# Average pooling over runs of four: where a group's rows lie in memory, and which queue stores them

## The chip, the cores and the metric

The kernel runs on one NeuronCore of a Trainium2 chip. The metric is the device time of one execution in microseconds (us); lower is better. A core has several engines with instruction streams of their own: VectorE (DVE in the profile), ScalarE (ACT), GpSimd (POOL), SyncE (SP) and TensorE (PE). Sixteen DMA engines move data between the chip's main memory (HBM) and the on-chip memory (SBUF, 128 partitions). An engine that issues a transfer puts it into its own DMA queue: here SP has one (q1 in the profile) and ScalarE another (q10), and both are served by the same sixteen DMA engines.

## The reference

```python
def setup_inputs():
    return {
        "x": np.random.randn(64, 256, 8192).astype(np.float32),
        "kernel_size": 4,
        "stride": 4,
    }

def reference(x, kernel_size, stride):
    batch, channels, length = x.shape
    out_len = (length - kernel_size) // stride + 1
    output = np.zeros((batch, channels, out_len), dtype=np.float32)
    for i in range(out_len):
        start = i * stride
        output[:, :, i] = np.mean(x[:, :, start : start + kernel_size], axis=2)
    return output
```

Every four neighbouring values of the input become their mean. Windows do not overlap and no window crosses a row, so the whole input may be treated as one long line of numbers: 536.87 MB in, 134.22 MB out.

## The kernel before

The input is cut into 64 blocks of 8.39 MB. A block is 128 partitions of RUN = 16384 numbers, 64 KB each, and one block is one contiguous stretch of HBM: partition p's 64 KB follow those of partition p-1 (`xb`, L35). Its result is 128 partitions of M = 4096 numbers, 16 KB each, again one contiguous stretch (`ob`, L36).

For each block, `load` (L41 to L45) issues one transfer on SP's queue into an input tile `xt`. There are two input tiles (L38), so a load has to wait until VectorE has finished with the block two before. `sums` (L47 to L56) is two additions on VectorE: L50 adds neighbours, 16384 to 8192 numbers, and writes over the first half of `xt`; L54 adds neighbours again, 8192 to 4096, and writes half of a result tile `r`. A result tile holds two blocks, and there are two of them (L39). `scale` (L58, L59) multiplies by 1/4 on ScalarE, in place.

The order around the stores:

- The blocks go in pairs (L68). In the first eight blocks (SINGLES, L11) each block is scaled and stored by itself, with 16 KB per partition, by ScalarE's queue (L73 to L75).
- From the ninth block on, a pair is scaled in one instruction of 128 x 8192 numbers (L77) and stored by one transfer of 4096 KB on ScalarE's queue (L78). The function `both` (L65) gives its place in HBM: two blocks, so two separate runs of 16 KB for each partition.
- The last pair but one is scaled after the last loads have been issued, and stored on SP's queue (L86, L87). The last two blocks are stored singly on SP's queue (L90, L95), the very last in two pieces: its load, sums, scale and store are cut by LAST (L12) into 10240 and 6144 numbers.

Waits between engines are inserted by the framework from the tiles that an instruction reads and writes. Each engine runs its instructions in the order written, so an instruction that waits holds up those behind it on that engine. SP does nothing but issue transfers.

Of the kernel before, what the change touches and what calls it, by code (L numbers as in the profile page):

```python
# [1 line left out]

# [4 lines left out]


RUN = 16384

SINGLES = 8  # L11
LAST = (10240, 6144)  # L12


@with_exitstack
def kernel(
    ctx: ExitStack,
    tc: tile.TileContext,
    x: bass.AP,
    kernel_size: bass.AP,  # L20
    stride: bass.AP,
    out: bass.AP,
):
    nc = tc.nc
    K, S = int(kernel_size), int(stride)
    assert K == S == 4
    B, C, L = x.shape
    P = nc.NUM_PARTITIONS
    dt = x.dtype
    M = RUN // K  # L30
    blocks = B * C * L // (P * RUN)
    assert blocks * P * RUN == B * C * L and L % K == 0 and blocks % 2 == 0
    assert sum(LAST) == RUN

    xb = x.rearrange("b c l -> (b c l)").rearrange("(n p m) -> n p m", p=P, m=RUN)  # L35
    ob = out.rearrange("b c l -> (b c l)").rearrange("(n p m) -> n p m", p=P, m=M)  # L36

    pin = ctx.enter_context(tc.tile_pool(name="xin", bufs=2))  # L38
    pout = ctx.enter_context(tc.tile_pool(name="res", bufs=2))  # L39

    def load(i, a=0, b=RUN, xt=None):  # L41
        if xt is None:
            xt = pin.tile([P, RUN], dt, name="xt")
        nc.sync.dma_start(out=xt[:, a:b], in_=xb[i][:, a:b])
        return xt  # L45

    def sums(o, xt, a=0, b=RUN):  # L47
        v = xt[:, a:b].rearrange("p (m k) -> p m k", k=2)
        h = xt[:, a : (a + b) // 2]
        nc.vector.tensor_tensor(  # L50
            out=h, in0=v[:, :, 0], in1=v[:, :, 1], op=mybir.AluOpType.add
        )
        w = h.rearrange("p (m k) -> p m k", k=2)
        nc.vector.tensor_tensor(  # L54
            out=o, in0=w[:, :, 0], in1=w[:, :, 1], op=mybir.AluOpType.add
        )  # L56

    def scale(o):  # L58
        nc.scalar.mul(o, o, 1.0 / K)  # L59

    def edges(cuts):
        at = [sum(cuts[:j]) for j in range(len(cuts) + 1)]
        return list(zip(at[:-1], at[1:]))

    def both(i):  # L65
        return ob[i : i + 2].rearrange("n p m -> p n m")

    for i in range(0, blocks - 2, 2):  # L68
        r = pout.tile([P, 2, M], dt, name="r")
        for h in range(2):  # L70
            xt = load(i + h)
            sums(r[:, h, :], xt)
            if i < SINGLES:  # L73
                scale(r[:, h, :])
                nc.scalar.dma_start(out=ob[i + h], in_=r[:, h, :])  # L75
        if SINGLES <= i < blocks - 4:
            scale(r[:])  # L77
            nc.scalar.dma_start(out=both(i), in_=r[:])  # L78

    n = blocks - 1  # L80
    t = pout.tile([P, 2, M], dt, name="r")
    xt = load(n - 1)
    xl = None
    for a, b in edges(LAST):
        xl = load(n, a, b, xl)
    scale(r[:])  # L86
    nc.sync.dma_start(out=both(n - 3), in_=r[:])  # L87
    sums(t[:, 0, :], xt)
    scale(t[:, 0, :])
    nc.sync.dma_start(out=ob[n - 1], in_=t[:, 0, :])  # L90
    for a, b in edges(LAST):
        o = t[:, 1, a // K : b // K]
        sums(o, xl, a, b)
        scale(o)
        nc.sync.dma_start(out=ob[n][:, a // K : b // K], in_=o)  # L95


# [1 line left out]
_INS = ['x', 'kernel_size', 'stride']  # L99
_OUTS = [((64, 256, 2048), 'float32')]  # L100

_NUMBERS = {'kernel_size': 4, 'stride': 4}


# [26 lines left out]
```

## Time and profile before

| what | value |
|---|---|
| median of 3 runs | 1554.86 us (1554.7 to 1556.03) |
| the profiled execution | 1554.4 us, of which its span 1552.6 us |
| VectorE busy | 839.7 us (54%) |
| ScalarE busy | 227.4 us (15%) |
| one L50 of 128 x 8192, one L54 of 128 x 4096 | 8692 ns, 4425 ns |
| one L59 of 128 x 4096, of 128 x 8192 | 3616 ns, 7029 ns |
| HBM read and written | 536.87 MB and 134.22 MB, 432 GB/s over the span |
| issue to landing, median: load | 35.1 us |
| issue to landing, median: store of 2048 KB, of 4096 KB on ScalarE's queue | 31.7 us, 52.0 us |
| issue to landing: store of 4096 KB on SP's queue (L87) | 33.0 us |

The span is the time that the trace covers; the execution's own time is 1.8 us longer. "Busy" counts computing instructions only. A DMA engine handles a transfer as a row of packets, and a packet here is one contiguous run in HBM and in one partition: 64 KB for a load's partition, 16 KB for a store's. In lists of instructions in order of time the columns are start, length, engine, line, operation, what it writes and reads, and in brackets the idle time before it with what ended it. In lists of waits they are who waited for whom, the sum in us, how many times, and the longest.

### The profile page before, as it was taken

To read this page: it belongs to the slowest core of one execution; us is meant where nothing else is said; L and a number is where in the kernel's file an instruction comes from. 1 tells how busy PE (TensorE), PEld (TensorE's weight loads), DVE (VectorE), ACT (ScalarE), POOL (GpSimd) and SP (SyncE) were. 2 spreads that over 40 slices of the span, in tenths; PEclk is the share of its full clock that TensorE was granted. 3 is DMA by queue.
4 is the path that set the end of the run, shared out by engine and by line. 5 is a ranking of instruction groups with operands and counts; after the bars stand their busy time and mean duration, and the time that the engine had idled before them with its cause. 6 is when DMAs were issued, how large, how long until landed. Compare 5 with 4: busy or idle time off the path is not lost.

```text
span 1552.6 us, 471 instructions
## 1 busy us (share of the span) xinstructions
DVE 839.7 (54%) x130; ACT 227.4 (15%) x39; POOL 0.2 (0%) x4
## 2 busy tenths in 40 slices
DVE  3646556546465464654646546455464554645646
ACT  1111101110111101111011110111101111011111
POOL 0000000000000000000000000000000000000000
DMA  9999999999999999999999999999999999999999
GB/s 417 420 434 438 439 439 439 412 445 444 413 433 435 443 438 439 432 424 429 439 438 433 437 434 419 439 432 438 439 419 434 434 437 439 441 423 442 422 440 400
DMA packets 18292, 671.12 MB, mean 432 GB/s; under 512 B 1649, under 2 KB 1649, under 8 KB 1777
## 3 DMA queue, kind: packets, MB, share of 16 engines
q1 hardware_dynamic: 10064, 545.26, 81.1%
q10 hardware_dynamic: 8224, 125.83, 18.9%
q14 instruction: 4, 0.02, 0.0%
HBM read 536.87 MB, written 134.22 MB: 432 GB/s over the span
## 4 chain that ended last, share of the span: by engine, by line
DMA 71%; DVE 28%; issue 0%; ACT 0%; DVEq 0%
DMA xt<-in_x_dram 71%; DVE xt L50 18%; DVE r L54 9%; ACT r L59 0%; DVEq L54 0%
## 5 line engine op out<-in xcount | busy, mean ns | idle before, releaser
L50 DVE TENSOR_TENSOR xt<-xt 128x8192 f32<-128x8192 f32 (+1 forms) x65 | 556.5, 8561 | 696.1 <-DMA xt<-in_x_dram 696.1
L59 ACT ACTIVATE r<-r 128x8192 f32<-128x8192 f32 (+3 forms) x38 | 226.2, 5951 | 1313.0 <-DVE r L54 1313.0
L54 DVE TENSOR_TENSOR r<-xt 128x4096 f32<-128x4096 f32 (+1 forms) x65 | 283.4, 4360 | 3.9
L59 ACT ACT_TABLE_LOAD x1 | 1.3, 1283 | 0.7 <-PEq L112 0.7
L112 POOL MEMSET const-bfloat16-1.0<- 128x1 bf16 x1 | 0.1, 101 | 0.0
L112 POOL MEMSET const-uint8-127<- 128x1 uint8 x1 | 0.1, 101 | 0.0
L112 POOL MEMSET const-float32-0.0<- 128x1 f32 x1 | 0.1, 98 | 0.2 <-issue 0.2
L112 POOL MEMSET const-float32-1.0<- 128x1 f32 x1 | 0.1, 98 | 0.0
## 6 DMA issues: line engine op xcount, KB each, us to landing
out_dram<-r ACTq DMA_DIRECT2D x26, 4096.0 KB, 52.0
out_dram<-r ACTq DMA_DIRECT2D x8, 2048.0 KB, 31.7
xt<-in_x_dram SPq DMA_DIRECT2D x1, 5120.0 KB, 23.1
out_dram<-r SPq DMA_DIRECT2D x1, 4096.0 KB, 33.0
xt<-in_x_dram SPq DMA_DIRECT2D x1, 3072.0 KB, 30.0
out_dram<-r SPq DMA_DIRECT2D x1, 2048.0 KB, 16.9
out_dram<-r SPq DMA_DIRECT2D x1, 1280.0 KB, 12.9
xt<-in_x_dram SPq DMA_DIRECT2D x63, 35.1
```

What stands on the lines that cost most here:

```text
L50: nc.vector.tensor_tensor(out=h, in0=v[:, :, 0], in1=v[:, :, 1], op=mybir.AluOpType.add)
L54: nc.vector.tensor_tensor(out=o, in0=w[:, :, 0], in1=w[:, :, 1], op=mybir.AluOpType.add)
L59: nc.scalar.mul(o, o, 1.0 / K)
L112: nc = _bacc.Bacc("TRN2", target_bir_lowering=False, num_devices=1)
```

## The change

Blocks are replaced by groups of two halves. A group is 128 partitions with 128 KB of contiguous input each; half h of a group is the h-th 64 KB of every partition. A load still moves 64 KB for each of 128 partitions, but the rows of one load lie 128 KB apart in HBM rather than 64 KB. The two results of a partition then lie side by side in HBM, 32 KB in one run, so that a whole group is stored with one run per partition.

The first four groups (eight halves) are stored by halves on ScalarE's queue, with 16 KB per partition, 32 KB apart. From the fifth group on, each half is scaled by itself, nothing is stored by ScalarE, and SP issues the group's store (`store`, 4096 KB, 32 KB per partition) in the next group, behind the load of that group's second half. The group and its tile are kept in `held` until then. The end is ordered as before: the last loads, the held group, the last group's first half, and its second half in two pieces, all on SP's queue.

```diff
-SINGLES = 8
+SINGLES = 4
...
-    xb = x.rearrange("b c l -> (b c l)").rearrange("(n p m) -> n p m", p=P, m=RUN)
-    ob = out.rearrange("b c l -> (b c l)").rearrange("(n p m) -> n p m", p=P, m=M)
+    xb = x.rearrange("b c l -> (b c l)").rearrange(
+        "(n p h m) -> n h p m", p=P, h=2, m=RUN
+    )
+    ob = out.rearrange("b c l -> (b c l)").rearrange(
+        "(n p m) -> n p m", p=P, m=2 * M
+    )
...
-        nc.sync.dma_start(out=xt[:, a:b], in_=xb[i][:, a:b])
+        nc.sync.dma_start(out=xt[:, a:b], in_=xb[g, h][:, a:b])
...
-    def both(i):
-        return ob[i : i + 2].rearrange("n p m -> p n m")
+    def store(g, r, a=0, b=2 * M):
+        nc.sync.dma_start(out=ob[g][:, a:b], in_=r[:, a:b])
 
-    for i in range(0, blocks - 2, 2):
-        r = pout.tile([P, 2, M], dt, name="r")
-        for h in range(2):
-            xt = load(i + h)
-            sums(r[:, h, :], xt)
-            if i < SINGLES:
-                scale(r[:, h, :])
-                nc.scalar.dma_start(out=ob[i + h], in_=r[:, h, :])
-        if SINGLES <= i < blocks - 4:
-            scale(r[:])
-            nc.scalar.dma_start(out=both(i), in_=r[:])
+    def half(g, r, h):
+        o = r[:, h * M : (h + 1) * M]
+        nc.scalar.dma_start(out=ob[g][:, h * M : (h + 1) * M], in_=o)
 
-    n = blocks - 1
-    t = pout.tile([P, 2, M], dt, name="r")
-    xt = load(n - 1)
+    held = None
+    for g in range(groups):
+        r = pout.tile([P, 2 * M], dt, name="r")
+        xt = load(g, 0)
+        sums(r[:, :M], xt)
+        scale(r[:, :M])
+        if g == groups - 1:
+            break
+        if g < SINGLES:
+            half(g, r, 0)
+        xt = load(g, 1)
+        if held is not None:
+            store(*held)
+        sums(r[:, M:], xt)
+        scale(r[:, M:])
+        if g < SINGLES:
+            half(g, r, 1)
+        else:
+            held = g, r
+
     xl = None
     for a, b in edges(LAST):
-        xl = load(n, a, b, xl)
-    scale(r[:])
-    nc.sync.dma_start(out=both(n - 3), in_=r[:])
-    sums(t[:, 0, :], xt)
-    scale(t[:, 0, :])
-    nc.sync.dma_start(out=ob[n - 1], in_=t[:, 0, :])
+        xl = load(g, 1, a, b, xl)
+    store(*held)
+    store(g, r, 0, M)
     for a, b in edges(LAST):
-        o = t[:, 1, a // K : b // K]
-        sums(o, xl, a, b)
-        scale(o)
-        nc.sync.dma_start(out=ob[n][:, a // K : b // K], in_=o)
+        a1, b1 = M + a // K, M + b // K
+        sums(r[:, a1:b1], xl, a, b)
+        scale(r[:, a1:b1])
+        store(g, r, a1, b1)
```

In the changed file `load` is at L45 to L49 (the transfer at L48), the two additions at L54 and L58, the scale at L63, and the transfers of `store` and `half` at L70 and L74.

More of the change, by code (lines that the diff above doesn't have):

```diff
@@ L30, with load @@
     M = RUN // K
-    blocks = B * C * L // (P * RUN)
-    assert blocks * P * RUN == B * C * L and L % K == 0 and blocks % 2 == 0
+    groups = B * C * L // (2 * P * RUN)
+    assert groups * 2 * P * RUN == B * C * L and L % K == 0
     assert sum(LAST) == RUN
-    xb = x.rearrange("b c l -> (b c l)").rearrange("(n p m) -> n p m", p=P, m=RUN)
-    ob = out.rearrange("b c l -> (b c l)").rearrange("(n p m) -> n p m", p=P, m=M)
+    xb = x.rearrange("b c l -> (b c l)").rearrange(
[4 more added lines that the diff above has]
+    )
     pin = ctx.enter_context(tc.tile_pool(name="xin", bufs=2))
     pout = ctx.enter_context(tc.tile_pool(name="res", bufs=2))
-    def load(i, a=0, b=RUN, xt=None):
+    def load(g, h, a=0, b=RUN, xt=None):
         if xt is None:
             xt = pin.tile([P, RUN], dt, name="xt")
-        nc.sync.dma_start(out=xt[:, a:b], in_=xb[i][:, a:b])
+        nc.sync.dma_start(out=xt[:, a:b], in_=xb[g, h][:, a:b])
         return xt
```

## The prediction

> **What bounds the kernel now.** I read the page's stripes and queues first, then the chain, then the waits of VectorE and of SP, then the order of time in the middle and at the end. The queues on the page:
>
> ```profile
> DMA  9999999999999999999999999999999999999999
> DMA packets 18292, 671.12 MB, mean 432 GB/s; under 512 B 1649, under 2 KB 1649, under 8 KB 1777
> q1 hardware_dynamic: 10064, 545.26, 81.1%
> q10 hardware_dynamic: 8224, 125.83, 18.9%
> ...
> DMA 71%; DVE 28%; issue 0%; ACT 0%; DVEq 0%
> ```
>
> The 16 DMA engines are full in every slice, and the shares of the two queues (q1 is SP's, q10 ACT's) add up to 100% of the span. The chain's 28% of VectorE is misleading: it follows single waits through two input buffers, and says nothing of whether the DMA engines had other work meanwhile. The waits:
>
> ```profile
> ACT r L59 <- DVE r L54: 1313.0, 38, 44.8
> DVE xt L50 <- DMA xt<-in_x_dram: 696.1, 63, 22.7
> ...
> SPq L44 <- DVE r L54: 817.2, 62, 13.2
> SPq L44 <- DMA xt<-in_x_dram: 660.1, 62, 21.1
> ```
>
> VectorE waits for 63 loads, 11 us each; ScalarE waits for VectorE. SP waits up to 13.2 us for the sums to free a buffer, but it then issues a load behind one still running. The middle, in order of time (start, length):
>
> ```profile
> 400.29 8.69 DVE L50 TENSOR_TENSOR xt<-xt 128x8192 f32<-128x8192 f32 x1 [11.14 <-DMA xt<-in_x_dram]
> 409.07 4.43 DVE L54 TENSOR_TENSOR r<-xt 128x4096 f32<-128x4096 f32 x1
> 424.43 8.69 DVE L50 TENSOR_TENSOR xt<-xt 128x8192 f32<-128x8192 f32 x1 [10.93 <-DMA xt<-in_x_dram]
> 433.15 4.43 DVE L54 TENSOR_TENSOR r<-xt 128x4096 f32<-128x4096 f32 x1
> 437.62 7.03 ACT L59 ACTIVATE r<-r 128x8192 f32<-128x8192 f32 x1 [41.40 <-DVE r L54]
> 444.67 0.38 ACTq L78 DMA_DIRECT2D out_dram<-r  x1
> 448.65 8.69 DVE L50 TENSOR_TENSOR xt<-xt 128x8192 f32<-128x8192 f32 x1 [11.07 <-DMA xt<-in_x_dram]
> ```
>
> A pair takes 48.36 us (400.29 to 448.65) for 16.78 MB in and 4.19 MB out: 434 GB/s. Loads alone run no faster: VectorE's first two starts, 22.73 and 42.06, are 19.33 us apart for 8.39 MB, again 434 GB/s. So reads, writes and mixtures share one rate, and only bytes, packets and gaps count.
>
> No view prints packets singly, so I read the trace's packet records themselves. On one engine the next packet starts 2.414 us after a 64 KB packet, 0.607 after 16 KB, 0.381 after 10 KB, 0.231 after 6 KB, and 0.006 after a semaphore write. Each engine serves 128/16 = 8 partitions, so a load is 8 packets of 64 KB and a pair's store 16 of 16 KB. One engine's sum: 63 whole loads are 504 x 2.414 = 1216.7; the last, of 40 KB and 24 KB pieces at 1.510 and 0.908, 19.3; 16 KB stores, 64 in the singles, 416 in 26 pairs and 24 at the end, 504 x 0.607 = 305.9; the two last pieces 4.9; 103 semaphores 0.6. Together 1547.4 us. The first packets start at 3.0 to 3.8 us and the last ends with the span, 1552.6. Everything slower than these steps sums to 1.3 us per engine, 0.7 of it in the very first packets, 0.5 spread over loads beside stores.
>
> **The change, part by part.** The sum is against the profiled execution: span 1552.6, whole 1554.4, so 1.8 lie around it. The median of the runs is 1554.86, 0.46 above that execution.
>
> *Packets.* 27 pairs (26 of L78, one of L87) go from 16 packets of 16 KB to 8 of 32 KB per engine. A packet's fixed part is (4 x 0.607 - 2.414)/3 = 4.7 ns, so 32 KB should step by 1.209 instead of 1.214. Saved: 27 x 8 x 4.7 ns = 1.0 us, straight off the full engines. No 32 KB packet is in the trace, hence bounds. From below: nothing saved. From above: the packets' recorded lengths, 611 and 2415 ns, overlap a little and give (4 x 611 - 2415)/3 = 9.7 ns, 2.1 us in all. I take 1.0, since starts and not lengths fill the time.
>
> *The order.* A pair is now load, load, store in SP's queue, where q10's packets alternated one by one with loads. The step from load to store within SP's queue exists at the end of the trace (24 KB packets of the last load, a semaphore, then 16 KB of L87) and shows no gap. The step from store to load is there only between two queues, 7106 times, at 0.2 ns over the plain step. In one queue it is not shown. Bounds: the gaps beside stores vanish (-0.5 us), or each of 27 switches costs what the slowest engine pays when it starts cold, 1.0 us over 2.414 for its first packet (0.7 on the mean of the engines), 27 x 1.0 = 27 us. I take 0: in every change of kind that the trace has, the next packet was ready.
>
> *SP's waits.* Count from the start of load (g,0) on the engines: it ends at 19.3, load (g,1) at 38.6, the store of g-1 at 48.3, where load (g+1,0) must be in the queue. SP issues load (g,1) when the sums of (g-1,1) are done. That block landed 9.7 before zero, and 13.2 of sums (8.69 + 4.43 + gaps) end at 3.5. Scale (g-1,1) follows, 3.62, and SP, which the store makes wait, issues it at about 7.5, needed at 38.6. Queued behind it is load (g+1,0), which waits for the sums of (g,0) anyway: 19.3 + 13.2 = 32.5, needed at 48.3. Margins of 16, 31 and 16 us; an issue (0.33 us) and the first load's lead (22.0 from issue to landing less 19.3) use 3 of them. So nothing starves. Without this cover a late load would cost its lateness per pair.
>
> *ScalarE and buffers.* Two scales of 3.62 replace one of 7.03: 0.2 us more per pair, hidden by 41 us idle before each. The store instruction leaves ScalarE (0.38). Buffer r of group g+1 waits for the store of g-1, which ends at 48.3, while L58 writes r only after load (g+1,0) at 67.6 and 8.7 more: covered by 28 us. Nothing is late next.
>
> *Start and end.* The singles keep queue, size and count. At the end 8.39 MB of stores still follow the last load, in the same order as L87, L90, L95, and the last piece's sums and scale (3.35 + 1.76 + 1.48) lie under the pair's 9.7. Change: 0.
>
> *Addresses.* Load rows are 128 KB apart instead of 64, single stores 32 instead of 16. The trace has only the closer rows. From below 0; from above every load packet as slow as the cold first ones, 504 x 0.7 = 353 us. I take 0: it is near the rows with all engines reading at once and no gap. The Trainium skill (DMA: Bandwidth & Descriptors, Latency and other measured facts) speaks against this edit: rows a large power of two apart read slower, 207 GB/s at 512 KiB where padded rows gave 214; no run here shows it, and its list starts at four times this distance. If 128 KB already lost those 3.3% of 64 x 19.33 us, the sum would be 41 us longer, about 1595.
>
> Sum: 1552.6 - 1.0 = 1551.6 span; 1553.4 execution; about 1553.9 as a median. What this measurement can tell from no change is about 0.2%, 3.1 us, so the forecast is no change, slightly on the fast side.
>
> **The rivals.**
> Store to load stalls (slower). The engine reads nothing ahead behind a store of its own queue, and each of 27 switches pays. For: the cold start's 0.7 us on the mean, and in the kernel before loads and stores came from separate queues. Against: no gap from load to store, nor between queues. Price 27 x 0.7 = 19: 1553.9 + 19 = 1573. It decides from (3.1 + 1.0)/27 = 0.15 us per switch.
> Spread rows read slower (slower). For: 16 engines walk 512 KB apart instead of 256 KB, in step. Against: the reads have no gap now. Four late steps in mid-run were 0.31, 0.37, 0.53 and 0.56 us; one such (0.44) per load and engine is 64 x 0.44 = 28: 1553.9 + 28 = 1582. It decides from 4.1/504 = 8 ns per packet. The rule of the Trainium skill above would be this case.
> SP starves (the change does not do what it says: the store sits in the queue but holds up loads). It needs a load over 13 us late; each us beyond costs 27 us. Say 1 us: 1581. The waits speak against it.
> More than packets is won. With the upper packet price and no gaps beside stores: 1554.86 - 2.1 - 0.5 = 1552.3, still within 0.2%. Beyond that only 0.7 us of cold start is left, so a real gain needs a step shorter than any in the trace.
>
> **How the numbers follow.** Forecast, with the stronger saving: 0.60. Stall at the switch 0.17, spread rows 0.15, starving 0.03; of these 0.35 a tenth or so stays under its deciding point. Faster by an effect the trace does not show: 0.05. So faster 0.05, same 0.63, slower 0.32. The likeliest case alone spans 1552.3 to 1555.5. The range starts at 1552.2 (both savings) and reaches to 1564, a switch at half its price (27 x 0.35 = 9.5): that leaves out about 0.16 above and 0.04 below.
>
> **What would show it.** Right: 27 SP stores of 4096 KB; q10 down to 16.8 MB; VectorE's L54 starts 19.3 and 29.0 us apart in turn, 48.32 per pair; 32 KB packets stepping by 1.209. A stall shows as more than 29.0 after each store with 19.3 intact; slow rows as more than 19.33 between a group's two loads; starving as SP waits ending after the store's packets. A pair over 48.5 us makes the prediction wrong.

## The result and the profile after

Over 20 runs each, the changed kernel takes 1556.65 us (1556.09 to 1558.43) and the one before 1554.64 us (1554.23 to 1556.27): ratio 1.0013, 95% interval [1.0007, 1.0019]. It is 2 us slower where 1 us faster was forecast. That lies within 0.2% and within the range, but outside the likeliest case's 1552.3 to 1555.5. The profiled execution took 1557.28 us, its span 1555.5.

The page of the changed kernel, queues and then transfers (count, KB each, us from issue to landing):

```profile
DMA  9999999999999999999999999999999999999998
...
DMA packets 14835, 671.12 MB, mean 431 GB/s; under 512 B 1648, under 2 KB 1648, under 8 KB 1776
...
q1 hardware_dynamic: 13680, 654.32, 97.3%
q10 hardware_dynamic: 1152, 16.78, 2.5%
...
out_dram<-r SPq DMA_DIRECT2D x27, 4096.0 KB, 41.2
out_dram<-r ACTq DMA_DIRECT2D x8, 2048.0 KB, 31.7
```

The change does what it says: 27 stores went to SP's queue, and 3457 fewer packets carry the same bytes (27 x 128 of them by the stores). The DMA engines are as full as before and yet slower, 431 GB/s for 432. The waits say that nothing starves:

```profile
ACT r L63 <- DVE r L58: 1310.3, 65, 33.8
DVE xt L54 <- DMA xt<-in_x_dram: 698.8, 63, 22.6
...
SPq L48 <- DVE r L58: 817.1, 62, 13.2
SPq L48 <- DMA xt<-in_x_dram: 563.0, 62, 21.0
SPq L70 <- ACT r L63: 127.8, 30, 28.7
```

SP's wait for the sums is the old 817 us; its new wait for ScalarE (L70) lies where SP would have waited anyway. VectorE's wait for loads grew from 696.1 to 698.8 us, by 2.7, which is nearly the whole growth of the span (2.9). Where those 2.7 us are, the order of time shows. VectorE's first addition starts when a load has landed on all DMA engines; an early stretch and a late one:

```profile
498.43 8.69 DVE L54 TENSOR_TENSOR xt<-xt 128x8192 f32<-128x8192 f32 x1 [15.82 <-DMA xt<-in_x_dram]
...
517.80 8.69 DVE L54 TENSOR_TENSOR xt<-xt 128x8192 f32<-128x8192 f32 x1 [6.17 <-DMA xt<-in_x_dram]
...
546.85 8.69 DVE L54 TENSOR_TENSOR xt<-xt 128x8192 f32<-128x8192 f32 x1 [15.90 <-DMA xt<-in_x_dram]
...
566.78 8.69 DVE L54 TENSOR_TENSOR xt<-xt 128x8192 f32<-128x8192 f32 x1 [6.72 <-DMA xt<-in_x_dram]
...
595.85 8.69 DVE L54 TENSOR_TENSOR xt<-xt 128x8192 f32<-128x8192 f32 x1 [15.92 <-DMA xt<-in_x_dram]
```

```profile
1322.39 8.69 DVE L54 TENSOR_TENSOR xt<-xt 128x8192 f32<-128x8192 f32 x1 [15.86 <-DMA xt<-in_x_dram]
...
1341.73 8.69 DVE L54 TENSOR_TENSOR xt<-xt 128x8192 f32<-128x8192 f32 x1 [6.13 <-DMA xt<-in_x_dram]
...
1370.76 8.69 DVE L54 TENSOR_TENSOR xt<-xt 128x8192 f32<-128x8192 f32 x1 [15.88 <-DMA xt<-in_x_dram]
```

Late in the run the second half of a group lands 19.34 us after the first and the next group's first half 29.03 after that: 48.37 for the pair (1322.39 to 1370.76), nearly the forecast 48.32. Early on the step to the second half is 19.37 in one group and 19.93 in the next, while the step across the store is 29.05 and 29.07; the second of these pairs takes 49.00. So it is not the way back from the store to the load that costs, but the end of the second load, just ahead of the store, and only in a part of the run.

The packet records, read singly as for the prediction, give the whole sum. A record does not name its engine; the means below need no names, and the distances between engines further down come from the 16 semaphore writes that end a transfer. "Steps" is the sum of the undisturbed steps of one engine's packets, "late" what its packets took beyond these steps, both a mean of the 16 engines; then where the mean engine and the last engine end (us of the span):

```
kernel    steps     late   mean end   last end
before    1547.4     1.3     1550.7     1551.4
change    1546.4     3.4     1551.7     1554.2
```

1.0 us of steps is saved, as forecast (32 KB packets step by 1.209 us). Late packets cost 2.1 more on the mean engine, and the last engine is 2.5 behind the mean instead of 0.7; in both kernels the span ends 1.2 to 1.3 us after it. -1.0 + 2.1 + 1.8 is the span's 2.9. Of the 3.4 late, 1.5 sits on one packet in sixteen: the last load packet of a group ahead of the store. It takes up to 3.1 us instead of 2.418 where it is late, and the engines that arrive later are mostly the ones held up, so they fall further behind. The distance between the first and the last engine, taken from their semaphore writes at the end of a load:

```
before   255 us 0.43   449 0.43   594 1.01   836 1.01   1029 1.01   1464 1.02
change   256 us 0.43   420 1.40   575 2.70   807 4.04   1000 3.94   1484 4.05
```

Before, the engines stay 0.43 us apart until 560 us, when an instruction fetch (the page's queue q14, 8 KB, by one DMA engine) holds up one of them; after that they stay at 1.0, and at 1.6 in about every fourth load from 714 us on, with no drift. After the change they drift to 4 us by about 770 us and then stay there.

### The profile page after: what moved, and what is told of

It reads as the page before. It is cut to its first block, busy times and chain, and to the rows that moved or that the text cites. A ratio compares the mean times of both kernels' runs of the same rounds, so it can differ in the third digit from the quotient of the medians.

```text
span 1555.5 us, 473 instructions
## 1 busy us (share of the span) xinstructions
DVE 839.7 (54%) x130; ACT 232.9 (15%) x66; POOL 0.2 (0%) x4
## 4 chain that ended last, share of the span: by engine, by line
DMA 71%; DVE 28%; issue 0%; ACT 0%; DVEq 0%
DMA xt<-in_x_dram 71%; DVE xt L54 18%; DVE r L58 9%; ACT r L63 0%; DVEq L58 0%
## 5 line engine op out<-in xcount | busy, mean ns | idle before, releaser
L54 DVE TENSOR_TENSOR xt<-xt 128x8192 f32<-128x8192 f32 (+1 forms) x65 | 556.5, 8561 | 698.8 <-DMA xt<-in_x_dram 698.8
L63 ACT ACTIVATE r<-r 128x4096 f32<-128x4096 f32 (+1 forms) x65 | 231.6, 3564 | 1310.3 <-DVE r L58 1310.3
L58 DVE TENSOR_TENSOR r<-xt 128x4096 f32<-128x4096 f32 (+1 forms) x65 | 283.4, 4360 | 3.9
```

The source lines that it names most:

```text
L54: nc.vector.tensor_tensor(out=h, in0=v[:, :, 0], in1=v[:, :, 1], op=mybir.AluOpType.add)
L58: nc.vector.tensor_tensor(out=o, in0=w[:, :, 0], in1=w[:, :, 1], op=mybir.AluOpType.add)
```

## The experiments

Two theories at first: O, the order of the stores in SP's queue sets off the drift; L, the layout is slower. All ratios are to the kernel before in the same session, with 95% intervals.

### e1 to e4: the parts alone, more turns, another place

e1 keeps rows and 32 KB stores but has ScalarE issue them:

```diff
         xt = load(g, 1)
-        if held is not None:
-            store(*held)
         sums(r[:, M:], xt)
...
+        elif g < groups - 2:
+            nc.scalar.dma_start(out=ob[g], in_=r[:])
         else:
             held = g, r
```

> One part of the change alone: 128 KB rows and 32 KB stores, but each group's store goes to ScalarE's queue as soon as its second half is scaled, as before. Theory O (the order costs the time: in SP's queue every DMA engine turns from its last load packet to stores at about the same moment, and the late ones are held up; in the trace of the change all of the extra delay sits on the last 64 KB packet ahead of a store, 1.5 us per engine on the mean and 4 us between the first and the last engine at the end): no such delays here, only the packets saved, 1.0 us faster than before, 1553.6, ratio 0.9994. Theory L (the layout costs it: rows 128 KB apart, or 32 KB rows written side by side, are slower): as slow as the change, 1556.6, ratio 1.0013. Engines' ends within 1 us of each other by O, 4 us by L.

Measured: 1571.96 us, ratio 1.0109 [1.0095, 1.0123]. Neither theory had this. Four equal stretches of e1 (length; DVE, ACT and POOL busy us with counts; clock, DMA share, GB/s):

```profile
260.00:560.00 300.00, 165.68 (x26) 44.99 (x13) 0.00 (x0) 1.00 1.00 435
560.00:860.00 300.00, 157.40 (x24) 45.42 (x13) 0.00 (x0) 1.00 1.00 431
860.00:1160.00 300.00, 157.42 (x24) 43.39 (x12) 0.00 (x0) 1.00 1.00 426
1160.00:1460.00 300.00, 157.85 (x25) 43.39 (x12) 0.00 (x0) 1.00 1.00 425
```

The first stretch runs at 435 GB/s (the kernel before: 434 from 300 to 850 us), and then the rate falls for good. In the packets, from 590 us on, one or two load packets per engine around the start of each store take 2.6 to 3.5 us. What sets it off is followed up below; that it is not the rows as such, e5 shows.

e2 keeps the blocks and 16 KB runs of before and takes only the new order:

```diff
-        "(n p h m) -> n h p m", p=P, h=2, m=RUN
+        "(n h p m) -> n h p m", p=P, h=2, m=RUN
...
-        "(n p m) -> n p m", p=P, m=2 * M
+        "(n h p m) -> n p h m", p=P, h=2, m=M
```

(with each half's run addressed in the stores accordingly).

> The other part alone: blocks as before (64 KB rows, a pair stored as two runs of 16 KB per partition), but the pairs' stores in SP's queue behind the next pair's second load, as in the change. Theory O: the change's delay without its saving in packets, 1557.6, ratio 1.0019, with the delays on the last load packet before each store. Theory L: no delay, 1554.6, ratio 1.0000.

Measured: 1558.47 us, ratio 1.0025 [1.0015, 1.0035]. As O has it: the order alone costs 4.0 us. Its landings, early:

```profile
401.72 8.69 DVE L54 TENSOR_TENSOR xt<-xt 128x8192 f32<-128x8192 f32 x1 [16.20 <-DMA xt<-in_x_dram]
...
421.56 8.69 DVE L54 TENSOR_TENSOR xt<-xt 128x8192 f32<-128x8192 f32 x1 [6.63 <-DMA xt<-in_x_dram]
...
450.58 8.69 DVE L54 TENSOR_TENSOR xt<-xt 128x8192 f32<-128x8192 f32 x1 [15.87 <-DMA xt<-in_x_dram]
...
470.81 8.69 DVE L54 TENSOR_TENSOR xt<-xt 128x8192 f32<-128x8192 f32 x1 [7.02 <-DMA xt<-in_x_dram]
```

The same mark as in the change: 19.84 and 20.23 us to the second load instead of 19.34. The engines drift from 0.41 us (256 us) to 3.5 (710 us) and stay there to the end (3.8).

e3 stores each half by itself in SP's queue, so there are twice as many turns:

```diff
-        xt = load(g, 1)
         if held is not None:
-            store(*held)
+            store(*held, M, 2 * M)
+            held = None
+        xt = load(g, 1)
+        if g >= SINGLES and g < groups - 2:
+            store(g, r, 0, M)
```

> The layout of the change, but from the fifth group on each half is stored by itself in SP's queue, behind the load that follows it: twice as many turns from load to store, each with 8 packets of 16 KB per engine, and 27 semaphores more. Theory O as a price per turn (1.5 us over 27 turns is 0.06 us each on the mean engine, 0.15 on the last one): 54 turns, delays of 3 us on the mean engine and 8 on the last one, 1.0 more for the packets, 1562. Theory O as a drift that stops once the engines are 4 us apart (in the trace of the change there is none after the 18th group): no more than the change plus the packets, 1557.7. Theory L: 1557.7 too, but with e1 as slow as the change.

Measured: 1558.42 us, ratio 1.0025 [1.0016, 1.0035]. The doubled turns cost no more than e2's, which has the same 16 KB packets. The drift ends sooner instead: the engines are 4.1 us apart by 387 us, and flat for the remaining 1100 us. So the cost is not a price per turn but a distance that is reached once.

e4 moves the store ahead of the second load:

```diff
-        xt = load(g, 1)
         if held is not None:
             store(*held)
+        xt = load(g, 1)
```

> The change with one line moved: the held store is issued ahead of the load of the group's second half instead of behind it, so that SP's queue holds load, store, load. As many turns and packets as in the change; the turn now follows the first half's load. Theory O: the same time as the change, 1556.6, with the delays moved to the last packet of the first half. If it is the second half of the rows, or two loads in a row that bring the engines into step, the delays vanish and it takes 1553.6.

Measured: 1574.84 us, ratio 1.0122 [1.0105, 1.0139], 18 us above the slower of the two expectations. They had overlooked the lead, the time between the issue of a transfer and its turn; the order of time of e4:

```profile
639.84 3.62 ACT L63 ACTIVATE r<-r 128x4096 f32<-128x4096 f32 x1 [26.05 <-DVE r L58]
643.48 0.34 SPq L70 DMA_DIRECT2D out_dram<-r  x1
643.92 15.65 SPq L48 DMA_DIRECT2D xt<-in_x_dram  x2
646.00 8.69 DVE L54 TENSOR_TENSOR xt<-xt 128x8192 f32<-128x8192 f32 x1 [6.20 <-DMA xt<-in_x_dram]
```

The store waits for the scale of the half before and is issued at 643.48, when the load ahead of it has only 2.5 us to go (it lands at 646.00). Here the delays sit on store packets too (12.1 of 18.7 us late), nearly all on the last packet of a store, ahead of the next load: 317 store packets take more than 1.3 us, 1.77 in the median, where the others take 1.21. Whether the short lead or the place does it is for e9.

### e5 to e8: rows, pauses, time or address

After e1 the question was what is slow there: reading such rows (R), or stores that stop and start again (B). A store of 32 KB packets taken in turns with load packets is over after one load of two, where one of 16 KB packets lasts through both.

e5 stores halves from ScalarE's queue throughout, with the rows of the change:

```diff
-        if g < SINGLES:
+        if g < groups - 2:
             half(g, r, 0)
...
-        if g < SINGLES:
+        if g < groups - 2:
             half(g, r, 1)
-        elif g < groups - 2:
-            nc.scalar.dma_start(out=ob[g], in_=r[:])
```

> The rows of the change (loads 128 KB apart, half stores of 16 KB rows 32 KB apart), but each half stored by ScalarE's queue up to the last group but one, so that a store packet follows every load packet without pause, as before. e1 (same rows, same queue, 32 KB packets that last only half the time) took 17 us longer than before. Theory R (reading rows 128 KB apart is what is slow): slow again, 1565 or more. Theory B (stores that stop and start again are what is slow: the load packets ahead of a store's first packet took 2.6 to 3.4 us in e1 instead of 2.42, and none in the run before, where a store is always under way): as before, 1554.5, ratio 1.0000.

Measured: 1555.44 us, ratio 1.0005 [0.9996, 1.0014]: no difference that these runs resolve. Rows 128 KB apart are not what is slow. In its packets 1.5 us are late against 1.3 before.

e6 is the change with the addresses of the groups reversed (`groups - 1 - g` for `g` in loads and stores).

> The change with the groups taken in the opposite order, the 32nd group of HBM first; nothing else. In the change the late load packets fall into the groups from 300 to 850 us of the span and cease after that. Theory T (it depends on how far the engines have drifted apart, so on time since the start): the same stretch, 250 to 900 us, and the same time, 1556.6. Theory A (it depends on addresses, on which rows of input and output are open together): mirrored, mostly between 700 and 1250 us; the total near 1556.6 as well, so the profile decides.

Measured: 1557.87 us, ratio 1.0022 [1.0012, 1.0031]. The late packets fall mostly between 300 and 600 us again (0.72, 0.38 and 0.45 us per engine in these three hundreds, 0.16 or less in each one after), and the engines drift from 0.35 us at 285 to 3.7 at 710. So the addresses are not it. The total is 1.2 us above the change's; it was taken in another session, and the two were not run side by side.

e7 leaves all as before, but cuts each load into two transfers of half the columns (and the last block into two equal pieces):

```diff
-LAST = (10240, 6144)
+LAST = (8192, 8192)
...
-        nc.sync.dma_start(out=xt[:, a:b], in_=xb[i][:, a:b])
+        for c in range(a, b, RUN // 2):
+            d = min(b, c + RUN // 2)
+            nc.sync.dma_start(out=xt[:, c:d], in_=xb[i][:, c:d])
```

> The blocks and stores of before, but each load is cut into two transfers of half the columns, so its packets are 32 KB: a load is 16 packets per engine instead of 8, and a pair's 16 store packets, taken in turns with load packets, are gone after one load instead of two, so that stores stop for half the time, with no row 128 KB apart and no 32 KB store. Packets and semaphores alone cost 512 x 4.7 ns + 64 x 6 ns = 2.8 us: 1557.3. Theory B: stops and starts cost as in e1, 1565 to 1575. Theory R: 1557.3.

Measured: 1559.83 us, ratio 1.0034 [1.0021, 1.0047]. Its steps sum to 2.8 us more, as expected; the rest, 2.6, is mostly late packets (about 1.3) and a last engine about 0.8 further behind the mean. So stores that pause do cost, but far less than e1's 17 us. B in the size it was given falls.

e8 is e1 reversed in the same way as e6.

> e1 (rows of the change, 32 KB stores in ScalarE's queue) with the groups taken in the opposite order. In e1 there is no extra delay before 590 us and more and more after it. Theory T (time since the start, drift): the same course, little before 590 us, 1568 to 1574. Theory A (addresses): the delays fall into the first 950 us and the end is free of them.

Measured: 1567.74 us, a single run. No late packet from 250 to 500 us, the first after 560 and then 0.9 to 1.9 us per engine in every hundred: the course of e1, at the same times. Again time, not address.

### e9 and e10: the lead, and turns that come late

e9 holds two groups, so that the store between two loads is issued early:

```diff
-    held = None
+    held = []
...
-        r = pout.tile([P, 2 * M], dt, name="r")
         xt = load(g, 0)
+        if len(held) == 2:
+            store(*held.pop(0))
+        r = pout.tile([P, 2 * M], dt, name="r")
...
-        if held is not None:
-            store(*held)
...
-            held = g, r
+            held.append((g, r))
```

> The change, but a group's store is held for one load more, so SP's queue holds load, store, load as in e4, with the store issued some 30 us before the DMA engines reach it and the load behind it 16 us before. In e4 the store was issued 2.5 us before. Theory S (e4's 15 us and more come from the short lead of the store and what is behind it): as the change or e2, 1556 to 1558, with the engines 3.5 to 4 us apart after some ten turns and then no more. Theory P (a store between a group's halves is itself the bad place): as e4, 1568 to 1576.

Measured: 1557.40 us, ratio 1.0017 [1.0009, 1.0026]. The place is harmless; SP's waits for the scale are down to 4 in e9, where e4 has 30. First SP's waits in e9, then the same row of e4:

```profile
SPq L48 <- DVE r L58: 843.4, 62, 14.5
SPq L48 <- DMA xt<-in_x_dram: 619.8, 62, 21.1
SPq L70 <- ACT r L63: 40.9, 4, 20.1
```

```profile
SPq L70 <- ACT r L63: 880.1, 30, 33.5
```

No store packet of e9 takes more than 1.3 us. So e4's extra 17 us came with the short lead. What is left in e9 is the drift: 0.39 us at 256, 4.2 at 642, 4.3 at the end, and the late packet is now the last one of the first load, again the one ahead of the store.

e10 is the change with `SINGLES = 18`.

> The change with its first part made longer: the first 18 groups are stored by halves from ScalarE's queue, and only 13 turns from load to store follow in SP's queue, from about 920 us on. Theory D (each run of turns pushes late engines later until they are 3.5 to 4 us apart, after 8 to 17 turns, and costs no more after that): engines about 1 us apart up to 900 us, then 3 to 4; packets saved 13 x 37 ns = 0.5 us instead of 1.0; 1556.5. Theory E (an even price per turn, 3 us over 27 turns): 1554.5 - 0.5 + 13 x 0.11 = 1555.4. Theory T (only the time since the start counts, and delays cease after 850 us): no spreading, 1554.0.

Measured: 1557.98 us, ratio 1.0022 [1.0013, 1.0031], with 13 turns no less than with 27. The engines are at most 0.95 us apart up to 962 us, 2.29 at 1059, 3.45 at 1155, 3.8 at 1416. Theory D holds in the course, E and T fall. The size was 1.5 us above D's, which stays unexplained.

### e11 and e12: what sets off e1's delays

Both are e1 with a needless small load into a result tile that the sums overwrite, in e11 one of 8 KB and in e12 two of 16 KB; e12's form:

```diff
         xt = load(g, 1)
+        if g == 6:
+            for j in range(2):
+                nc.scalar.dma_start(out=r[j : j + 1, M:], in_=xb[0, 0][j : j + 1, 0:M])
         sums(r[:, M:], xt)
```

> e1 (rows of the change, 32 KB stores in ScalarE's queue) with one more transfer, 8 KB into one partition of a result tile that is overwritten later, issued by ScalarE near 290 us: it occupies one DMA engine for 0.3 us. In e1 and e8 the engines stay 0.5 and 0.4 us apart without any delay until an instruction fetch of 8 KB takes one engine at 560 us; the delays begin with the next store. Theory N (one engine out of step is what sets them off): they begin at 300 us, six groups earlier, at about 0.3 to 0.8 us a group, 2 to 5 us more than e1's 1572. Theory T (time since the start): they begin at 590 us, 1572 as e1.

Measured: 1567.49 us, ratio 1.0084 [1.0070, 1.0097]. Inconclusive: the transfer is in the trace at 288.2 us, but the engines were 0.33 us apart before it and 0.34 after. The delays begin after 560 us as in e1.

> e11 again with two transfers of 16 KB instead of one of 8 KB, each on one DMA engine, since e11's 0.3 us fell on an engine that was ahead and left the 16 engines 0.34 us apart as before. 1.2 us on one engine is more than the engines are apart, so it must break their step near 290 us. Theory N (one engine out of step sets off e1's delays): they begin with the next stores at 300 to 350 us, 4 to 5 groups' delays more than e11, 1569 to 1572 against its 1567.5, and load packets in the stretch 300 to 560 us are late. Theory T (time since the start, or the fetch at 560 us itself): the engines are further apart from 290 us on, but no load packet is late before 560 us, 1567 to 1568.

Measured: 1574.58 us, ratio 1.0123 [1.0106, 1.0140]. The engines are 0.41 us apart at 255 us and 1.31 at 304, where one of them is 0.9 us behind the next and the other 15 stand as before. The next two stores start when they do in e1. The same four stretches of e12:

```profile
260.00:560.00 300.00, 164.05 (x26) 43.39 (x12) 0.00 (x0) 1.00 1.00 432
560.00:860.00 300.00, 158.99 (x25) 46.71 (x13) 0.00 (x0) 1.00 1.00 427
860.00:1160.00 300.00, 157.42 (x24) 43.69 (x13) 0.00 (x0) 1.00 1.00 425
1160.00:1460.00 300.00, 157.41 (x24) 43.39 (x12) 0.00 (x0) 1.00 1.00 424
```

432 instead of 435 GB/s already in the first stretch, and the decline comes 200 us sooner: late load packets of 0.4 to 0.7 us per group begin at 390 us, where e1 has none before 590. They start with the third store behind the nudge, not with the first, but well ahead of the fetch at 563 us. So one engine out of step was enough to set them off, in one profile of one kernel.

## Why the prediction was wrong, point by point

- **The bound and the packets** held. The DMA engines are full, waits of SP and ScalarE are covered as the margins had it, and a 32 KB packet steps by 1.209 us: the sum of the steps fell by the 1.0 us of that term. As a difference of times this cannot be seen alone; change and e2, which differ in it and in the rows, are 1556.65 and 1558.47 us in two sessions, ratios 1.0013 and 1.0025 with overlapping intervals. Two readings were off without weight in the sum: in the trace's own times the first packets start at 1.7 to 2.5 us, not at 3.0 to 3.8, and the last ends 1.2 us before the span does; and a 64 KB packet's recorded length is 2418 ns in the median, not 2415, which makes the upper price 8.7 ns and 1.9 us.
- **The order, taken at 0, is the step that failed.** The prediction read the turn from load to store from its single occurrence in SP's queue, at the end of the trace, found no gap and priced all 27 at nothing. One turn does not show it: in the change the first one, in the sixth group, has no gap either. The turns hold up late engines from about 320 us on, until the 16 engines are 4 us apart, and the order by itself costs 4.0 us (e2). It costs that once, whether there are 13, 27 or about 54 turns (e10, e2, e3). With e2's 4.0 us in place of 0 the prediction's sum would have been 1552.6 - 1.0 + 4.0 = 1555.6 us; the measured span is 1555.5.
- **The rival "store to load stalls"** had the right neighbourhood and the wrong turn. The step from 32 KB stores back to a load shows 0 to 1 ns over the plain step; the late packet is ahead of the store. Its price per switch would have grown with the number of switches, which e3 and e10 exclude. Only in e4, where a store is issued late, is the turn back to a load slow: there 317 of the last store packets take 1.77 us in the median instead of 1.21.
- **Addresses, at 0,** held: e5 is at 1.0005 [0.9996, 1.0014]. The Trainium skill (DMA: Bandwidth & Descriptors, Latency and other measured facts), by which copies of rows large powers of two apart are slower, may hold from the 512 KiB that it lists; at 128 KB the 3.3% of the prediction's estimate is excluded here. Two of the four late steps from which the rival "spread rows" was priced, 0.56 and 0.31 us, stand right behind an instruction fetch on the same engine, so they said nothing of rows.
- **The signs** did not tell the causes apart. A pair of 49.00 us came, over the 48.5 that was to show the prediction wrong; but the longer step was the one between a group's two loads, with the step across the store near 29.0, and this was to be the sign of slow rows. e2, with the rows of before, shows the same sign, so it belongs to the order.
- **"Everything slower than these steps sums to 1.3 us"** was right for the kernel before and was taken for a limit on what may happen after. The sum was made for a mean engine. The kernel ends with the last one, and how far it lags was not a term of it: 0.7 us before, 2.5 after.

Not settled: why a load packet is late when a store is next, why the late engines are hit more, and why it ends near 4 us. Nor is it separated which of 64 KB load packets, 32 KB store packets and pauses together makes e1 so much worse than e7. None of the kernels run is faster than the one before; the lowest of them is e5.

## What to carry to other kernels

In a kernel whose DMA engines are always full, count not only bytes and packets but how far the engines run apart: a load has landed, and the kernel has ended, when the slowest of sixteen is done. In these runs, packets of loads and stores that alternate without a pause from two queues kept the engines within 2 us at the end of every load (the kernel before and e5); long phases of one kind, in one queue or by larger store packets, let them drift. And a change in the order of transfers that repeats dozens of times should not be priced from one occurrence at the end of a trace.

## What the runs showed of the hardware

- A fetch of 8 KB of instructions, carried by the same DMA engines, set one of them back by 0.9 us in the kernel before (0.31 for the fetch and 0.56 on the next load packet; the engines went from 0.43 to 1.01 us apart at 560 us), and the distance did not close again. In e1 a fetch of that kind at 560 us stands at the start of a decline from 435 to 425 GB/s, and e12's nudge of two 16 KB packets brought it on earlier.
- A packet costs 4.7 ns beyond its bytes on an engine, from 6 KB to 64 KB, with 36.8 ns per KB (of 1000 bytes), worked out from steps of 0.231 us for 6 KB, 0.607 for 16 KB, 1.209 for 32 KB and 2.414 for 64 KB.
- A store issued 2.5 us ahead of its turn in a queue, with a load behind it, cost about 17 us in 27 turns (e4 against e9, 1574.84 against 1557.40 us), although the DMA engines stand at 90% or more in every slice of e4's page.
